# Mixer of a hybrid encoder step on Trainium2: three selection rounds a step for the first scored tile, and one weight split moved behind a group of projections

## The chip, the cores and the metric

The kernel runs on one core of a Trainium2 chip. What counts is the device time of one execution in microseconds (us). The kernel before took 1135.36 us, the median of three runs (1133.62 to 1137.08). One more execution was profiled; every duration of a single instruction below comes from that one.

The engines are named as the profile names them: PE is the matrix engine (its weight loads are listed apart as PEld), DVE the vector engine, ACT the scalar engine, POOL the GpSimd engine, SP the engine whose queue issues most of the DMA transfers.

## The reference, cut to what matters

One encoder layer is computed for 512 prompt tokens and 32 sample tokens that share the weights: a feed-forward block, a mixer, a second feed-forward block, each closed by a layernorm. The change is in the mixer. Its input projection and its sparse attention are, in short:

```python
z = jnp.einsum('btd,de->bte', h, w_in)          # retention q,k,v,gate | attention q,k,v | indexer q, key, head weights
s = jnp.einsum('bqhd,bsd->bqhs', iq, ik) * (IDX_DH ** -0.5)
index_score = jnp.einsum('bqh,bqhs->bqs', iw, jax.nn.relu(s))
index_score = jnp.where(admissible[None], index_score, NEG)
_, idx = lax.top_k(index_score, topk)           # topk = 128 prompt, 136 sample
logits = jnp.einsum('bqhd,bqkhd->bqhk', q, kg) * (ATT_DH ** -0.5)
p = jax.nn.softmax(logits, axis=-1)             # over the selected keys alone
```

Each query token scores all keys that it may see, keeps the best 128 (136 for the sample tokens), and attends to those. Beside it four retention heads run (a chunked recurrence with its own q, k, v).

## The kernel before, in words

**Layout.** Activations lie transposed: 128 partitions of the model width by 544 tokens, in two halves of 272 columns. Every weight is split in two parts (a rounded part and the remainder, "hi" and "lo"), so that a product of a 128 x 1024 weight block with one half is 24 matmuls. PE does these almost without a break; that is where nearly all of the time goes.

**Weights.** A weight block is fetched by SP's queue into a raw tile (`wr_w`, three buffers), rounded by ACT into the hi part (`wh_w`, line 131, five buffers), and the lo part is made in one of two ways: by a subtraction on DVE (line 141), or by ACT (line 138) and an adding DMA that POOL issues (line 139). `ensure(n)` sees to it that n weights ahead of the next one have been split; `next_w` takes the next. The order in which the program asks for a split sets where the fetch stands in SP's queue, where the rounding stands on ACT and where the subtraction stands on DVE. The input projection has 33 weight blocks. The first four (the index key with the head weights, and three of the four index queries) are taken together; the fifth is the last index query; the sixth is the q of the first retention head. The fifth and the sixth have their lo part made on DVE.

**Around the first projections.** The last products of the first feed-forward block (`dn`), the layernorm of each half and the four leading projections overlap. `k_outer` runs the four leading projections together over one half, and lets other jobs go on after every second part of the width. For the second half, the sums S and Q (lines 264 and 265) go through two matmuls (`pm`, `pv`), which PE holds between the first and the second quarter of the leading projections of the first half; then DVE and ACT make the normalised and split input `h` of that half (lines 332 to 367).

**Jobs and steps.** Side work is written as jobs that are resumed at every tick of the program; a tick comes after each product of a block with a half, or so. `topk()` is such a job. It selects in rounds of eight: `max` finds the eight largest of each row (line 1125), `match_replace` marks them in the row (line 1126). Tiles 1, 2 and 3 of 128 queries have rows of 256, 384 and 512 scores and take 16 rounds each; the sample tile 's' has rows of 544 and takes 17. (Tile 0 has 128 keys and needs none.) After its rounds a tile's row is turned into a mask (line 1129) that the attention adds to its logits (line 1293). The `rate` in `topk` is the number of rounds in one step. As the job goes straight on with the next tile, everything behind a tile that is done in fewer steps moves up as well.

**Attention.** `attention()` is another job. For a pair of heads c and a group n of query tiles it forms logits (`lg`) in two PSUM banks, one for each head of the pair; group 0 holds tiles 0 and 1, group 1 tile 2, group 2 tile 3. DVE adds the mask and takes the maximum (line 1293), which frees the bank; ACT and DVE do the softmax (lines 1285 to 1290). The name `lg` has two banks in all, so that the logits of the next group wait until the masks of this group have been added.

**What sets the order.** Instructions of one engine stand in one list, and the rows of the trace start in the order of that list. A scheduler orders the lists when the kernel is built, from the order of the program, priorities and given dependencies. So a change of one number in `topk` moves rows of DVE and ACT over a long stretch.

## Time and profile before

| what | value |
|---|---|
| median of three runs | 1135.36 us |
| lowest and highest run | 1133.62, 1137.08 us |
| the profiled execution's own time | 1134.79 us |
| its span, first to last instruction | 1133.0 us |
| PE busy | 1110.3 us (98%) |
| DVE busy | 850.6 us (75%) |
| ACT busy | 636.8 us (56%) |
| granted PE clock, mean over the span | 0.993 |

A row of the timeline reads: start in us from the start of the span, duration of the row in us, engine, line, operation, out<-in, shape, how many instructions the row merges, and in brackets the idle time of the engine just ahead and what ended it. The table by windows gives for each stretch the busy time of every engine, then the PE clock that was granted (1.00 is full speed), the share of the DMA engines that was busy and GB/s.

### The profile page before, as it was taken

How to read it: one execution, taken by the hardware profiler on the slowest of the kernel's cores; microseconds unless marked ns; L12 is line 12 of the kernel's file. 1: busy time of each engine (PE TensorE's matmuls, PEld its weight loads, DVE VectorE, ACT ScalarE, POOL GpSimd, SP SyncE). 2: the span in 40 equal slices, each digit the busy share in tenths (PEclk: the TensorE clock that was granted, in tenths of full speed). 3: DMA queues.
4: the chain of work that ended last, by engine and by line, in shares of the span. 5: the costliest groups of instructions: out<-in, count | busy, mean ns of one | idle time of the engine just before them, and what ended most of it. 6: DMA issues, size and time to landing. Idle time of an engine off the chain costs nothing.

```text
span 1133.0 us, 22791 instructions
## 1 busy us (share of the span) xinstructions
PE 1110.3 (98%) x9059; PEld 1079.8 (95%) x9059; DVE 850.6 (75%) x1766; ACT 636.8 (56%) x1116; POOL 196.3 (17%) x217
## 2 busy tenths in 40 slices
PE   8999999999999999999989999999999999999995
PEld 7999999999999999989988899999999999999995
DVE  5578898788779799677898887799799876920416
ACT  3645656754334444865556668646666666653524
POOL 0111111122010303422110101100111111151110
PEclk9999999999999999999989999999999999999998
DMA  9798878997977556744946587862888677488842
GB/s 359 274 270 220 224 191 218 260 269 246 320 208 171 143 217 151 155 117 127 276 91 199 123 270 204 206 194 34 231 221 229 167 174 184 129 226 176 175 83 80
DMA packets 71164, 221.18 MB, mean 195 GB/s; under 512 B 8624, under 2 KB 12848, under 8 KB 71056
## 3 DMA queue, kind: packets, MB, share of 16 engines
q1 hardware_dynamic: 49456, 151.02, 37.9%
q0 software_dynamic: 21456, 68.56, 33.6%
q8 instruction: 71, 1.16, 0.4%
q14 instruction: 37, 0.30, 0.1%
q10 hardware_dynamic: 144, 0.14, 0.0%
HBM read 208.09 MB, written 9.58 MB: 192 GB/s over the span
## 4 chain that ended last, share of the span: by engine, by line
PE 86%; DVE 7%; DMA 5%; ACT 1%; issue 1%; SPq 0%; DVEq 0%; ACTq 0%
PE dn L77 26%; PE pA L77 16%; PE in L77 13%; PE gu L77 11%; PE pB L77 8%; PE pC L77 4%; DMA we_raw<-in_w_e 3%; PE gu_e L77 2%; DVE m L1125 1%; DVE wk L1126 1%; DMA aqk<-rp 1%; PE isc L77 1%; PE ro L77 1%; PE lg L77 1%; PE pt L80 1%
## 5 line engine op out<-in xcount | busy, mean ns | idle before, releaser
L77 PE MATMUL dn<-hid,wh_w 128*128 128x272 f32 x2112 | 267.1, 288 | 0.0
L77 PEld LDWEIGHTS dn<-hid,wh_w 128*128 128x128 f32 x2112 | 265.5, 188 | 0.4 <-DMA wh_w<-in_w_dn 0.3
L77 PE MATMUL in<-h,wh_w 128*128 128x272 f32 x1392 | 188.5, 293 | 0.0
L77 PEld LDWEIGHTS in<-h,wh_w 128*128 128x128 f32 x1392 | 178.5, 190 | 5.1 <-issue 2.9
L131 ACT CAST wh_w<-wr_w 128x1024 fp32r<-128x1024 f32 (+1 forms) x102 | 103.0, 1014 | 99.6 <-PE dn L77 83.7
L77 PE MATMUL gu<-h,wh_w 128*128 128x272 f32 x960 | 121.1, 288 | 0.0
L77 PEld LDWEIGHTS gu<-h,wh_w 128*128 128x128 f32 x960 | 120.6, 188 | 0.0
L589 DVE SCALAR_TENSOR_TENSOR ca<-wc,cz,ca 128x1024 f32<-128x1024 f32 x84 | 107.4, 1298 | 0.0
L77 PE MATMUL pA<-hs,wh_s 128*128 128x272 f32 x720 | 100.2, 288 | 0.0
L77 PEld LDWEIGHTS pA<-hs,wh_s 128*128 128x128 f32 x720 | 93.7, 188 | 0.0
L138 ACT ACTIVATE wh_w<-wh_w 128x1024 fp32r<-128x1024 f32 (+1 forms) x80 | 81.5, 1023 | 1.5
L286 DVE SCALAR_TENSOR_TENSOR xs<-dn,C,xs 128x272 f32<-128x272 f32 (+2 forms) x24 | 9.0, 403 | 80.3 <-PE dn L77 80.3
L693 POOL DMA_DIRECT2D wh_g<-in_w_gu x30 | 26.1, 870 | 240.8 <-ACT wh_g L692 164.1
L727 ACT COPY s<-pA 128x272 f32<-128x272 f32 x90 | 34.5, 383 | 53.7 <-PE pA L77 53.1
L139 POOL DMA_DIRECT2D wh_w<-in_w_dn x32 | 28.2, 880 | 174.9 <-ACT wh_w L138 131.8
L716 DVE TENSOR_TENSOR wh_s<-wr_g,wh_s 128x1024 fp32r<-128x1024 f32 x30 | 36.7, 1225 | 19.4 <-ACT wh_s L715 19.4
L77 PE MATMUL pA<-h,wh_g 128*128 128x272 f32 x360 | 50.1, 288 | 0.0
L77 PE MATMUL pB<-hs,wh_u 128*128 128x272 f32 x360 | 49.8, 287 | 0.0
L77 PE MATMUL pC<-h,wh_g 128*128 128x272 f32 x360 | 49.8, 287 | 0.0
L77 PE MATMUL pB<-hs,wh_s 128*128 128x272 f32 x360 | 49.8, 287 | 0.0
L77 PE MATMUL pA<-h,wh_s 128*128 128x272 f32 x360 | 49.7, 287 | 0.0
L715 ACT CAST wh_s<-wr_g 128x1024 fp32r<-128x1024 f32 x30 | 31.5, 1051 | 30.2 <-DVE wr_g L711 30.2
(331 smaller groups left out, 2051.5 us busy)
## 6 DMA issues: line engine op xcount, KB each, us to landing
wc<-in_w_cond SPq DMA_DIRECT2D x52, 512.0 KB, 6.8
wr_w<-in_w_in SPq DMA_DIRECT2D x33, 512.0 KB, 5.2
wr_g<-in_w_gu SPq DMA_DIRECT2D x30, 512.0 KB, 3.5
wr_u<-in_w_gu SPq DMA_DIRECT2D x30, 512.0 KB, 4.4
wh_g<-in_w_gu POOLq DMA_DIRECT2D x30, 512.0 KB, 6.6
wr_w<-in_w_dn SPq DMA_DIRECT2D x32, 448.0 KB, 4.3
wh_w<-in_w_in POOLq DMA_DIRECT2D x27, 512.0 KB, 6.6
wr_w<-in_w_gu SPq DMA_DIRECT2D x24, 512.0 KB, 7.2
```

The lines of the kernel that those rows point to most:

```text
L77: ordered("pe", nc.tensor.matmul(*a, **kw))
L80: ordered("pe", nc.tensor.transpose(*a))
L131: c = nc.scalar.copy(hi[:, :n, :], raw[:, :n, :])
L138: nc.scalar.mul(lo[:, :n, :], hi[:, :n, :].bitcast(F32), -1.0)
L139: nc.gpsimd.dma_start(lo[:, :n, :], src, accum_op=ALU.add)
L589: got = nc.vector.scalar_tensor_tensor(acc, ws[n], c, acc, op0=ALU.mult, op1=ALU.add)
L693: nc.gpsimd.dma_start(lo, src, accum_op=ALU.add)
L715: pin(nc.scalar.copy(W[f][:, 0], raw[f]))
L716: pin(nc.vector.tensor_tensor(W[f][:, 1], raw[f], W[f][:, 0].bitcast(F32), op=ALU.subtract))
L727: pin(nc.scalar.copy(s, ps))
L1125: behind(behind(nc.vector.max(m8, w), "pe"), "norm")
L1126: nc.vector.match_replace(w, in_to_replace=m8, in_values=w, imm_value=MARK)
```

## The change

Three edits. In the mixer's head, `ensure(2)` becomes `ensure(1)`: ahead of the leading projections one weight is split (the fifth), no longer two. Inside the loop over the halves, `ensure(2)` now stands behind `k_outer`, so that the sixth weight is split behind the products of the first half (in the second pass it finds nothing to do). And in `topk`, tile 1 takes three rounds a step where it took two; tiles 2 and 3 keep two, the sample tile keeps its own rhythm.

```diff
     hls = [next_w(0) for c in range(4)]
-    ensure(2)
+    ensure(1)
     misc = unit("misc")
@@
     for i, (a, b) in enumerate(HALVES):
         accs = [(hls[c], bank(("aaao", "lltt")[i][c], "in")[:, :HT]) for c in range(4)]
         k_outer(accs, h, i)
+        ensure(2)
         for c, (_, ps) in enumerate(accs):
             taken((z, *qs)[c])(ps, a, b)
@@
     def topk():
-        for t, rate in ((1, 2), (2, 2), (3, 2), ('s', 1)):
+        for t, rate in ((1, 3), (2, 2), (3, 2), ('s', 1)):
```

No instruction is added or taken out on any engine, and PE's list and POOL's list keep their order. What moves stands on DVE, ACT and SP. (Behind line 1003 the lines of the changed kernel have numbers higher by one.)

**First place: DVE at the layernorm ahead of the projections.** The subtraction for the sixth weight stood between two steps of the layernorm of the first half:

```order
 L265 TENSOR_TENSOR Q<-Q,sq 128x272
 L338 SCALAR_TENSOR_TENSOR pv<-lnz 128x272
-L141 TENSOR_TENSOR wh_w<-wr_w,wh_w 128x1024
 L339 SCALAR_TENSOR_TENSOR pv<-pv,lnz 128x272
 L341 SCALAR_TENSOR_TENSOR lny<-pv,lny 128x272
```

It is gone from there. A little further on in the same list, S and Q are the sums of the second half, h_5 to h_7 the last parts of the input of the first half:

```order
 L367 SCALAR_TENSOR_TENSOR h_4_4815<-ht,B_3755,h_4_4815 128x272
-L364 SCALAR_TENSOR_TENSOR ht<-xa_3229,G_3754,lny 128x272
+L367 SCALAR_TENSOR_TENSOR h_5_4816<-ht,B_3755,h_5_4816 128x272
 L364 SCALAR_TENSOR_TENSOR ht<-xa_3230,G_3754,lny 128x272 x2
-L367 SCALAR_TENSOR_TENSOR h_5_4816<-ht,B_3755,h_5_4816 128x272
+L264 TENSOR_TENSOR S<-S,xa_3230 128x272
+L265 TENSOR_TENSOR Q<-Q,sq 128x272
 L367 SCALAR_TENSOR_TENSOR h_6_4817<-ht,B_3755,h_6_4817 128x272
 L367 SCALAR_TENSOR_TENSOR h_7_4818<-ht,B_3755,h_7_4818 128x272
-L264 TENSOR_TENSOR S<-S,xa_3230 128x272
-L265 TENSOR_TENSOR Q<-Q,sq 128x272
```

S and Q now stand ahead of the last two parts of h; they stood behind them. The subtraction itself comes back behind the first two instructions of a side job (`ca`, the sums of a conditioning vector):

```order
 L607 TENSOR_SCALAR ca_0_4927<-wc_0_4929,cz 128x1024
 L607 TENSOR_SCALAR ca_1_4928<-wc_0_4929,cz 128x1024
+L141 TENSOR_TENSOR wh_w<-wr_w,wh_w 128x1024
 L609 SCALAR_TENSOR_TENSOR ca_0_4927<-wc_1_4930,cz,ca_0_4927 128x1024
 L609 SCALAR_TENSOR_TENSOR ca_1_4928<-wc_1_4930,cz,ca_1_4928 128x1024
```

That is behind the whole layernorm of the second half.

**Second place: SP's queue over the same stretch.** The raw tile of the sixth weight was fetched with the five ahead of it:

```order
-L74 DMA wr_w<-in_w_in 128x1024 x6
+L74 DMA wr_w<-in_w_in 128x1024 x5
 L74 DMA misc<-in_csm 128x12
 L74 DMA misc<-in_cikT 128x512
 L74 DMA tabA<-in_ropes 128x1088
 L74 DMA tabR<-in_ropes 128x1088
-L74 DMA wc_4_4955<-in_w_cond 128x1024
-L74 DMA wc_5_4957<-in_w_cond 128x1024
-L74 DMA wr_w<-in_w_in 128x1024 x4
+L74 DMA wc_4_4950<-in_w_cond 128x1024
+L74 DMA wc_5_4952<-in_w_cond 128x1024
+L74 DMA wr_w<-in_w_in 128x1024 x5
```

It now stands behind the small tables and two conditioning weights, ahead of four other weights.

**Third place: DVE ahead of the first masked logits.** `wk_5279` holds tile 3 here and `wk_5278` the sample tile; aks and aqs are the lo parts of the keys and queries of head pair 0; the last row is the first masking. Before, its last twelve rows were:

```order
L1126 MATCH_REPLACE wk_5279<-m_7099,wk_5279 128x512
L1125 MAX m_7137<-wk_5279 128x8
L1126 MATCH_REPLACE wk_5279<-m_7137,wk_5279 128x512
L1125 MAX m_7140<-wk_5279 128x8
L1125 MAX m_7182<-wk_5278 128x8
L1126 MATCH_REPLACE wk_5279<-m_7140,wk_5279 128x512
L1126 MATCH_REPLACE wk_5278<-m_7182,wk_5278 128x544
L1129 TENSOR_SCALAR wk_5279<-wk_5279 128x512
L1125 MAX m_7185<-wk_5278 128x8
L1132 MEMSET wk_5279 64x64
L1126 MATCH_REPLACE wk_5278<-m_7185,wk_5278 128x544
L1293 ISA Pu,mx<-lg,wk_5279 128x128
```

Now they are:

```order
L1127 MATCH_REPLACE wk_5278<-m_7058,wk_5278 128x544
L962 TENSOR_TENSOR aks<-aqk,aks 128x512
L962 TENSOR_TENSOR aqs<-aqk,aqs 128x512
L1126 MAX m_7116<-wk_5278 128x8
L1127 MATCH_REPLACE wk_5278<-m_7116,wk_5278 128x544
L1126 MAX m_7154<-wk_5278 128x8
L1127 MATCH_REPLACE wk_5278<-m_7154,wk_5278 128x544
L1126 MAX m_7194<-wk_5278 128x8
L1127 MATCH_REPLACE wk_5278<-m_7194,wk_5278 128x544
L1126 MAX m_7197<-wk_5278 128x8
L1127 MATCH_REPLACE wk_5278<-m_7197,wk_5278 128x544
L1294 ISA Pu,mx<-lg,wk_5279 128x128
```

Counted in the two lists from the statistics of the fourth retention head (`bst`) to that first masking: 10 rounds of tile 3 and 2 of the sample tile before, 4 of tile 3 and 6 of the sample tile now. Tile 3 is finished ahead of aks, and four rounds of the sample tile follow on aqs where six and a half of tile 3 and two of the sample tile stood. From the third to the fourth head's statistics the list held 6 rounds of tile 2 and 6 of tile 3, and holds 12 of tile 3 now; the earlier stretches take up the rest, three rounds at a time where two stood.

## The prediction

> **What bounds the kernel now.** I read the page first, then what PE waited for, then PE's own timeline around those waits, and last what DVE did meanwhile.

> ```profile
> span 1133.0 us, 22791 instructions
> PE 1110.3 (98%) x9059; PEld 1079.8 (95%) x9059; DVE 850.6 (75%) x1766; ACT 636.8 (56%) x1116; POOL 196.3 (17%) x217
> PE 86%; DVE 7%; DMA 5%; ACT 1%; issue 1%; SPq 0%; DVEq 0%; ACTq 0%
> PE lg L77 <- DVE mx L1293: 3.5, 2, 3.2
> PE pm L77 <- DVE S L264: 1.5, 1, 1.5
> ```

> PE is busy for 98% of the span and carries 86% of the chain that ended last. Its list and its matmuls stay as they are, so the change can win only what PE waits or runs slowly. The list of what each engine waited for (total, times, longest) has two entries in the mixer of over 1 us for PE, and both are waits for DVE: 3.2 us at the logits (`lg`) and 1.5 us at the layernorm's sums (`pm`).

> First the logits, in PE's timeline and in the windows:

> ```profile
> 582.16 3.26 PE L77 MATMUL in<-h,wh_w 128*128 128x272 f32 x24
> 588.64 1.73 PE L77 MATMUL lg<-aks,aqs 64*128 64x384 f32 x6 [3.22 <-DVE mx L1293]
> 590.30 5.31 PE L77 MATMUL in<-h,wh_w 128*128 128x272 f32 x24
> 612.10 0.80 PE L77 MATMUL lg<-aks,aqs 64*128 64x384 f32 x6
> ...
> 408.00:410.00 2.00, 1.05 (x5) 0.90 (x6) 1.24 (x4) 0.53 (x2) 0.00 (x0) 1.00 1.01 409
> ...
> 588.00:590.00 2.00, 1.36 (x6) 1.10 (x6) 2.00 (x14) 1.72 (x7) 0.00 (x0) 0.51 0.30 57
> 596.00:598.00 2.00, 2.00 (x19) 1.64 (x16) 1.33 (x3) 1.50 (x5) 0.00 (x0) 1.00 0.37 139
> ```

> PE is through at 585.42 and starts the logits of group 1 at 588.64. The wait costs more than its length: behind it the granted clock is 0.51, and 1.00 again in the window from 596. Six logits take 1.73 us where the same six take 0.80 at 612.10, and 24 projections 5.31 us instead of 3.26. So the place costs 3.22 + 0.93 + 2.05 = 6.2 us. The wait of 1.5 us at `pm` left the clock alone (1.00 in the window from 408).

> [...]

> **Why DVE is late there.**

> ```profile
> 562.22 0.49 DVE L1268 BATCH_NORM_STATS2 bst<-rsB 128x6 f32<-128x128 f32 x2 [3.23 <-ACT rsB L1238]
> 575.84 0.69 DVE L962 TENSOR_TENSOR aqs<-aqk,aqs 128x512 fp32r<-128x512 f32 x1 [0.37 <-ACT aqs L961]
> 577.23 0.69 DVE L1125 MAX8 m<-wk 128x8 f32<-128x512 f32 x1
> 578.75 0.69 DVE L1125 MAX8 m<-wk 128x8 f32<-128x512 f32 x1
> 586.22 0.72 DVE L1125 MAX8 m<-wk 128x8 f32<-128x544 f32 x1
> 587.05 0.71 DVE L1126 MATCH_REPLACE8 wk<-m,wk 128x544 f32<-128x544 f32 x1
> 587.68 0.28 DVE L1293 CUSTOM_DVE_ANT_0 Pu<-lg,wk 128x128 f32<-128x128 f32 x1
> 588.16 0.41 DVE L1293 CUSTOM_DVE_ANT_0 Pu<-lg,wk 128x256 f32<-128x256 f32 x1
> 588.57 0.41 DVE L1293 CUSTOM_DVE_ANT_0 Pu<-lg,wk 128x256 f32<-128x256 f32 x1
> ```

> The banks of group 0 come free when its four maskings are done, the first bank at 588.57 and the second at 588.98. DVE begins them at 587.68 because selection rounds stand ahead of them: from the fourth head's statistics at 562.22 it works on without a gap but for the 0.37 us ahead of aqs. It is a queue of work, not a late input.

> **The attention's part, step by step.** A round of tile 3 takes 578.75 - 577.23 = 1.52 us; a round of the sample tile, from the two rows of 544, 587.05 + 0.71 - 586.22 = 1.54 us. By the two lists shown above, the stretch from `bst` to the first masking loses 6 rounds of tile 3 (9.1 us) and gains 4 of the sample tile (6.2 us), and the 0.37 us ahead of aqs goes, since DVE now comes to aqs later than its input: 3.3 us earlier, 584.4. Counted the other way, on from aqs: that had four and a half rounds of tile 3 ahead of it in the stretch, and now has four, two of the sample tile and tile 3's mask (some 0.5 us): 3.1 + 0.5 - 0.8 - 0.4 = 2.4 us later, at 578.2; with its own 0.69 and four rounds the masking starts at 585.1. I take 584.7: the first bank is free at 585.6, the second at 586.0. PE wants the first at 585.42 and the second one matmul later, so about 0.5 us of wait stays, and a wait of three times that has left the clock alone. The logits behind that, at 590.30 + 5.31 = 595.6 before, come at 585.42 + 0.5 + 0.8 + 3.1 = 589.8: a gain of **5.8 us**. The ends: nothing, if DVE is no earlier, and 6.2.

> That DVE has room for the rounds which come earlier is seen in its own waits from 436 to 562:

> ```profile
> DVE rqk L951 <- ACT sw L950: 12.8, 13, 1.9
> DVE bst L1268 <- ACT rsB L1238: 3.7, 3, 1.2
> ...
> 560.33 0.39 PE L77 MATMUL ro<-rv,rqk 128*128 128x128 f32 x2
> ```

> It stood idle for 12.8 us ahead of 13 evacuations and 3.7 us ahead of three statistics, and then 3.23 us ahead of the fourth (the row at 562.22), all of them waits for ACT. Rounds moved up fall into such gaps. Where they don't fit, rows behind them slip: between the third and the fourth statistics six rounds of tile 3 replace six of 384 columns, at most 6 x 1.52 / 4 = 2.3 us more, and 3.23 us of gap stand at the end. The nearest need of PE there is the last state of the retention, used at 560.33 and written by the last DVE row but one ahead of 562.22 - 3.23 = 559.0; 2.3 us on top would make PE wait some 0.7 us. Part of it goes into the gaps, so I take 0; the ends are 0 and 0.7. And aqs, done at 578.9, is asked for at 581.28 (a row below): 2.4 us of cover.

> What is late next: DVE has gained 3 us there, PE 5.8, so their next meeting tightens.

> ```profile
> 581.28 0.95 PE L77 MATMUL lg<-aks,aqs 64*128 64x128 f32 x12
> 596.67 0.17 DVE L1289 RECIPROCAL rl<-l 128x1 f32<-128x1 f32 x1 [1.58 <-ACT Pu L1287]
> 604.54 0.68 DVE L962 TENSOR_TENSOR aqs<-aqk,aqs 128x512 fp32r<-128x512 f32 x1
> 606.18 0.95 PE L77 MATMUL lg<-aks,aqs 64*128 64x128 f32 x12
> 639.31 1.19 PE L77 MATMUL lg<-aks,aqs 64*128 64x384 f32 x6 [0.26 <-DVE mx L1293]
> ```

> PE wants head pair 1 at 606.18 - 5.8 = 600.4. DVE's list from the first masking to that aqs is as before: 605.22 - 587.68 = 17.5 us, with 1.58 us in it for an exponential that stood on ACT behind an evacuation of the slow PE block. In ACT's new list the evacuation stands behind it, so 15.9 us: ready at 600.6. With the handing over I take **0.5 us** lost; the ends are 0 and, with the 1.58 us kept, 1.8. The wait of 0.26 us at 639.31 goes, since the sample tile's last rounds no longer stand ahead of it: **0.3 us** won.

> **The layernorm's part.**

> ```profile
> 391.88 12.52 PE L77 MATMUL dn<-hid,wh_w 128*128 128x272 f32 x96
> 404.24 3.18 PE L77 MATMUL in<-h,wu_w 128*128 128x272 f32 x24
> 408.95 0.73 PE L77 MATMUL pm<-S,cm 128*128 128x272 f32 x2 [1.52 <-DVE S L264]
> ...
> 399.15 1.22 DVE L141 TENSOR_TENSOR wh_w<-wr_w,wh_w 128x1024 fp32r<-128x1024 f32 x1
> 400.29 0.44 DVE L339 SCALAR_TENSOR_TENSOR pv<-pv,lnz 128x272 f32<-128x272 f32 x1
> 407.22 1.32 DVE L367 SCALAR_TENSOR_TENSOR h<-ht,B,h 128x272 fp32r<-128x272 f32 x3
> 408.46 0.43 DVE L264 TENSOR_TENSOR S<-S,xa 128x272 f32<-128x272 f32 x1
> ```

> PE has done its first 24 projections at 407.42 and waits until 408.95 for S, which ends at 408.89. The subtraction at 399.15 holds DVE's list up by 400.29 - 399.15 = 1.14 us, and two of the three h rows at 407.22 now stand behind S, 0.83 us. Without both S could end at 406.9. It also needs the last `dn` product, which PE ends at 404.40; from there two updates, two rows of h and the two ahead of h follow, six rows of at most 0.41 us, and S itself: 407.3 at the latest. That is ahead of 407.42, so **1.5 us** go. The ends: 0, if something else holds the list, and 1.5, since no more is waited.

> The subtraction and the fetch are paid later.

> ```profile
> 403.80 21.07 SPq L74 DMA_DIRECT2D wr_w<-in_w_in  x4
> 430.37 1.48 SPq L1010 DMA_DIRECT2D rp<-ix  x2
> 426.82 12.04 DVE L609 SCALAR_TENSOR_TENSOR ca<-wc,cz,ca 128x1024 f32<-128x1024 f32 x10
> ```

> With all 1.5 us earlier, DVE is through `ca`'s first two rows at 425.3 and the subtraction at 426.5, while PE comes to the sixth weight behind ten blocks of 24 from 404.24 on, at about 436. It lies beside PE's work and costs nothing: 9 us of cover. In SP's queue the fetch of the ninth weight waits for that subtraction (for the raw buffer), and the index key's gathers (line 1010) stand behind it. Before, the fourth of the fetches at 403.80 was out by 424.87; now the last two go out at 426.5, ahead of 428.9, when the gathers are due.

> **The sum**, against the profiled 1134.79 us: - 5.8 - 1.5 + 0.5 - 0.3 = - 7.1, so 1127.7. The median stands 0.6 above that execution: **1128.3 us** is the forecast.

> **The rivals.**

> The wait moves to head pair 1: 1.8 us remain there, or the clock falls as well. With the clock kept the time is 1.3 more, 1129.6; halved, it is another 0.93 + 2.05, 1132.6. For it: both engines meet there within 0.2 us by the sum above. Against: such a wait is nearer to the 1.52 us that left the clock alone. Chance 0.10, half for each.

> The rounds do nothing for PE, and only the layernorm's 1.5 us come: 1133.9. For it: the stretch starts with a wait for ACT that the change leaves in place. Against: DVE idles no more than 0.37 us in the 25 us behind it. Chance 0.06.

> The half clock fell on the profiled execution and not on most of the timed ones. A before without it loses 3.2 us at the logits and not 6.2, so the gain is 3.0 smaller: 1131.3. The three runs lie 3.5 us apart, which fits either way. Chance 0.06. [...]

> Slower: SP's queue now depends on DVE. If the moved subtraction ended late, the fetch that waits for its buffer would hold the gathers behind it, and with them the index scores and every round. It would have to end behind all of `ca`, 426.82 + 12.04 = 438.9, which makes the gathers 10 us late; what covers the first microseconds is not in these rows, so I count 4 us of it, and PE waits 6 us with a halved clock behind, 9 us in all: 1137.3. It decides from about 433 on. The list puts the subtraction ahead of ten of the twelve `ca` rows, so 0.04.

> The change does what the sum says: 0.74, with 1126 to 1130 as its own range.

> **How the numbers follow.** Faster by over 0.3% (3.4 us, about what a measurement of this kernel tells from no change) is below 1132.0: the forecast's 0.74, 1129.6 (0.05) and 1131.3 (0.06), less 0.01 for spread: 0.84. Within 0.3%: 1132.6, 1133.9 and that rest, 0.12. Slower: 0.04. The range 1125.5 to 1132.0 leaves out those 0.16 above; its low end is the sum with all 6.2 us, without the 0.5, and 1.7 us for the distance of the lowest run from the median.

> **What would show it.** Right: no wait of PE over 0.6 us at `lg` or `pm`; the clock at 1.00 all through the mixer; the first masking begun at most 0.5 us ahead of PE's call for the bank; aqs of pair 1 the next wait, under 1 us. Wrong: a clock near 0.5 anywhere between 570 and 640, a wait of PE at `ro` or at the first `lg`, or the gathers of line 1011 begun behind 429.

## The result

The changed kernel takes 1126.94 us (median of five runs, 1126.58 to 1128.46) beside 1136.76 us for the kernel before (five runs): a ratio of 0.9922, with a 95% interval of 0.9907 to 0.9938. Two later comparisons of the same pair gave 0.9933 (0.9920 to 0.9945) and 0.9942 (0.9929 to 0.9956). The forecast was 1128.3 with a range of 1125.5 to 1132.0. The profiled execution took 1126.58 us. One of the five runs in the last of these comparisons took 1342.37 us at a granted clock of 0.751 and is left out of every figure here.

From the page of the changed kernel, and then from the list of what PE waited for (total, times, longest):

```profile
span 1124.7 us, 22790 instructions
PE 1107.7 (98%) x9059; PEld 1077.4 (96%) x9059; DVE 848.5 (75%) x1766; ACT 637.4 (57%) x1116; POOL 196.1 (17%) x217
PE idle L77 <- POOL zeros L496: 1.2, 1, 1.2
PE c L77 <- DVE modT L523: 0.7, 1, 0.7
PE pt L80 <- ACT Pu L1414: 0.6, 1, 0.6
```

The span is 8.3 us shorter. Both entries of the mixer that named DVE, 3.5 us at `lg` and 1.5 us at `pm`, are gone from the list; what is left of the mixer there is 0.6 us for ACT at `pt`, which the kernel before had too. Next PE's timeline at the places that the prediction spoke of, and two stretches of the table by windows (the PE clock is the third number from the end):

```profile
404.35 3.19 PE L77 MATMUL in<-h,wu_w 128*128 128x272 f32 x24
407.37 0.62 PE L77 MATMUL pm<-S,cm 128*128 128x272 f32 x2
580.45 3.26 PE L77 MATMUL in<-h,wh_w 128*128 128x272 f32 x24
583.83 1.20 PE L77 MATMUL lg<-aks,aqs 64*128 64x384 f32 x6
584.96 3.30 PE L77 MATMUL in<-h,wh_w 128*128 128x272 f32 x24
598.83 0.95 PE L77 MATMUL lg<-aks,aqs 64*128 64x128 f32 x12
631.63 0.79 PE L77 MATMUL lg<-aks,aqs 64*128 64x384 f32 x6
...
584.00:586.00 2.00, 2.00 (x14) 1.52 (x15) 2.00 (x13) 1.71 (x7) 0.00 (x0) 1.00 1.06 162
588.00:590.00 2.00, 2.00 (x17) 1.44 (x16) 2.00 (x8) 1.94 (x6) 0.00 (x0) 1.00 0.00 0
```

PE's list is the same in both kernels, so one matmul can be followed from trace to trace. `pm` starts at 407.37 where it started at 408.95. The logits of group 1 start at 583.83 (588.64), those of head pair 1 at 598.83 (606.18), those of group 1 of head pair 2 at 631.63 (639.31). So the lead over the kernel before is 1.6 us behind the layernorm, 4.8 us when the banks come free, 7.35 us at head pair 1 and 7.7 us at head pair 2. The clock is 1.00 all through the mixer, and the 24 projections behind the logits take 3.30 us, not 5.31.

Last DVE, with the rows that answer to those shown of before:

```profile
406.74 0.44 DVE L264 TENSOR_TENSOR S<-S,xa 128x272 f32<-128x272 f32 x1
424.04 1.22 DVE L141 TENSOR_TENSOR wh_w<-wr_w,wh_w 128x1024 fp32r<-128x1024 f32 x1
560.51 0.49 DVE L1269 BATCH_NORM_STATS2 bst<-rsB 128x6 f32<-128x128 f32 x2 [2.26 <-ACT rsB L1239]
576.05 0.69 DVE L962 TENSOR_TENSOR aqs<-aqk,aqs 128x512 fp32r<-128x512 f32 x1
582.87 0.28 DVE L1294 CUSTOM_DVE_ANT_0 Pu<-lg,wk 128x128 f32<-128x128 f32 x1
583.76 0.41 DVE L1294 CUSTOM_DVE_ANT_0 Pu<-lg,wk 128x256 f32<-128x256 f32 x1
598.06 0.68 DVE L962 TENSOR_TENSOR aqs<-aqk,aqs 128x512 fp32r<-128x512 f32 x1
```

From the fourth head's statistics to the first masking DVE took 587.68 - 562.22 = 25.5 us before and takes 582.87 - 560.51 = 22.4 us now. PE asks for the first bank at 580.45 + 3.26 = 583.71; the second is released at 584.17. What is left of the wait lies there: 0.12 us ahead of the row at 583.83, and 0.40 us inside it (1.20 us against 0.80 for the same six matmuls), 0.5 us in all.

### The profile page after: what moved, and what is told of

Its sections match the earlier page's. It is cut to its first block, busy times and chain, and to the rows that moved or that the text cites. A ratio compares the mean times of both kernels' runs of the same rounds, so it can differ in the third digit from the quotient of the medians.

```text
span 1124.7 us, 22790 instructions
## 1 busy us (share of the span) xinstructions
PE 1107.7 (98%) x9059; PEld 1077.4 (96%) x9059; DVE 848.5 (75%) x1766; ACT 637.4 (57%) x1116; POOL 196.1 (17%) x217
## 4 chain that ended last, share of the span: by engine, by line
PE 89%; DVE 5%; DMA 4%; issue 1%; ACT 1%; SPq 0%; DVEq 0%; POOL 0%; POOLq 0%; ACTq 0%
PE dn L77 26%; PE pA L77 16%; PE in L77 16%; PE gu L77 11%; PE pB L77 8%; PE pC L77 4%; DMA we_raw<-in_w_e 3%; PE gu_e L77 2%; PE pt L80 1%; PE po L77 1%; PE lg L77 1%; PE isc L77 1%; DMA wh_w<-in_w_dn 1%; PE ro L77 1%; DVE m L1126 1%
## 5 line engine op out<-in xcount | busy, mean ns | idle before, releaser
L77 PE MATMUL dn<-hid,wh_w 128*128 128x272 f32 x2112 | 267.0, 288 | 0.1
L77 PEld LDWEIGHTS dn<-hid,wh_w 128*128 128x128 f32 x2112 | 265.5, 188 | 0.5 <-DMA wh_w<-in_w_dn 0.3
L77 PE MATMUL in<-h,wh_w 128*128 128x272 f32 x1392 | 186.5, 291 | 0.0
L77 PEld LDWEIGHTS in<-h,wh_w 128*128 128x128 f32 x1392 | 176.4, 188 | 4.9 <-issue 2.9
L77 PE MATMUL gu<-h,wh_w 128*128 128x272 f32 x960 | 121.1, 288 | 0.0
L77 PEld LDWEIGHTS gu<-h,wh_w 128*128 128x128 f32 x960 | 120.6, 188 | 0.0
L77 PE MATMUL pA<-hs,wh_s 128*128 128x272 f32 x720 | 100.3, 288 | 0.0
L77 PEld LDWEIGHTS pA<-hs,wh_s 128*128 128x128 f32 x720 | 93.7, 188 | 0.0
L77 PE MATMUL pA<-h,wh_g 128*128 128x272 f32 x360 | 50.1, 288 | 0.0
L77 PE MATMUL pB<-hs,wh_u 128*128 128x272 f32 x360 | 49.8, 287 | 0.0
L77 PE MATMUL pC<-h,wh_g 128*128 128x272 f32 x360 | 49.8, 287 | 0.0
L77 PE MATMUL pB<-hs,wh_s 128*128 128x272 f32 x360 | 49.8, 287 | 0.0
L77 PE MATMUL pA<-h,wh_s 128*128 128x272 f32 x360 | 49.7, 287 | 0.0
```

What stands on the lines that cost most here:

```text
L77: ordered("pe", nc.tensor.matmul(*a, **kw))
```

## Experiments

All times are medians; the ratio is to the kernel before, run beside each group on the same chip (1134.60, 1134.88 and 1134.49 us in the three groups).

| kernel | us | ratio (95%) |
|---|---|---|
| both (the change) | 1126.64 | 0.9933 (0.9920 to 0.9945) |
| weight_only | 1133.19 | 0.9990 (0.9981 to 0.9999) |
| rounds_only | 1129.53 | 0.9955 (0.9942 to 0.9967) |
| weight_later | 1128.77 | 0.9947 (0.9933 to 0.9960) |
| masks_4 | 1129.60 | 0.9953 (0.9940 to 0.9967) |
| masks_8 | 1133.01 | 0.9985 (0.9975 to 0.9995) |
| tile2_instead | 1127.98 | 0.9939 (0.9925 to 0.9952) |
| vector_splits | 1127.29 | 0.9932 (0.9919 to 0.9944) |
| both_again (the change) | 1128.05 | 0.9942 (0.9929 to 0.9956) |
| tile3_instead | 1134.16 | 0.9999 (0.9990 to 1.0008) |
| tile1_four | 1127.14 | 0.9935 (0.9923 to 0.9947) |
| four_and_splits | 1126.29 | 0.9930 (0.9916 to 0.9943) |

### The two parts, each alone

The change itself, once more:

> The changed kernel itself, beside the two that follow. The two profiles differ by 8.3 us (1133.0 and 1124.7 of span). If that is all that the change does, the time falls by 8.3 us, with 7.5 to 9.1 for the spread of the medians. If part of the 9.8 us between the two medians measured so far is real, some 1.5 us come from something that the two profiles do not show.

Measured: 8.0 us less than the kernel before, within what was expected. Nothing here asks for more than the 8.3 us of the two profiles; the 9.8 us between the first two medians are not repeated.

The weight alone:

```diff
-    ensure(2)
+    ensure(1)
@@
         k_outer(accs, h, i)
+        ensure(2)
```

> Only the two edits on the sixth weight; tile 1 keeps two rounds a step. The theory of the prediction: the wait of 1.52 us for S goes and nothing else, so 1.7 us less than the kernel before (the two profiles are 1.66 us apart at that point), and the wait of 3.2 us at the logits of group 1 stays as long as it was, with the granted clock near 0.5 behind it. Rival: DVE is tied to something there that does not come earlier, so that PE, 1.7 us earlier, waits 4.9 us at the logits and the time does not move.

The rounds alone:

```diff
-        for t, rate in ((1, 2), (2, 2), (3, 2), ('s', 1)):
+        for t, rate in ((1, 3), (2, 2), (3, 2), ('s', 1)):
```

> Only the third edit: three rounds a step in tile 1; the sixth weight is split where it was. The theory of the prediction: 3.1 us of wait at the logits and 2.7 us of half clock go, and some 0.5 us at the logits of group 1 of head pair 2, so 6.2 to 6.6 us less than the kernel before; the wait of 1.5 us for S stays. Rival, that the half clock fell on the profiled execution and not on most timed ones: 3.0 us less of a gain, 3.5 us. With the other kernel the gains add up to that of both edits, to within 1 us.

Measured: 1.4 us less for the weight, 5.1 us less for the rounds, 6.5 us together against 8.0 for both edits. That is 1.5 us apart where 1 us was expected, and the rounds alone gave 1.1 us less than the 6.2 expected; the intervals allow equality (the product of the two ratios is 0.9945). PE's timeline of weight_only and then of rounds_only around the logits, and of the same two at `pm` of the first half:

```profile
588.35 1.73 PE L77 MATMUL lg<-aks,aqs 64*128 64x384 f32 x6 [3.21 <-DVE mx L1294]
590.00 5.14 PE L77 MATMUL in<-h,wh_w 128*128 128x272 f32 x24
...
588.10 1.20 PE L77 MATMUL lg<-aks,aqs 64*128 64x384 f32 x6
...
392.50 0.73 PE L77 MATMUL pm<-S,cm 128*128 128x272 f32 x2 [1.68 <-DVE S L264]
...
392.47 0.75 PE L77 MATMUL pm<-S,cm 128*128 128x272 f32 x2 [1.73 <-DVE S L264]
```

With the weight alone the wait at the logits is 3.21 us, as before, and the clock is at 0.50 behind it: DVE and PE both come earlier by what the layernorm won, and the rival (a wait of 4.9 us) is out. With the rounds alone the wait ahead of the logits is gone. A gain of 3.5 us, as the rival has it in which the half clock fell on the profiled execution alone, lies outside the interval (3.7 to 6.6 us). The mean granted clock of the timed runs points the same way: 0.993 or 0.994 in 13 of the 15 runs of the kernel before and 0.995 in two; 0.996 or 0.997 in ten of the 14 runs of the changed one and 0.995 in four. The 6.8 us at half speed in 1133 take 0.003 off the mean. The mean also holds the slow clock at the start of the kernel, which lasts 4.4 to 10.4 us in the profiles, so a single 0.995 does not tell which it was.

But both profiles hold a wait that neither edit explains: 1.7 us at `pm` of the first half, near 391, where the kernel before and the changed kernel have none. It is taken up below (vector_splits). In rounds_only's profiled execution, the slowest of its five, that place costs 3.5 us against the changed kernel's trace: 1.9 of waiting and 1.6 of half clock behind it. How many of the other runs have it is not known.

### Does DVE's list alone decide?

Rows added to DVE's list ahead of the maskings that free the banks (k is 4, then 8):

```diff
+                    for _ in range(k if (c, n, t) == (0, 0, 0) else 0):
+                        masked(Pt, ps[:, a:b], work[t], mx)
                     masked(Pt, ps[:, a:b], work[t], mx)
```

> The changed kernel, with the masking of tile 0 of head pair 0 done four times more for each head of the pair (the same sums into the same place): eight more rows, which start 0.21 us apart in the profile of the changed kernel, ahead of the two maskings that free the banks. They add 1.7 us to DVE's list between PE's first logits and the logits of group 1, and nothing else moves on DVE. The theory: DVE's list alone decides when PE gets the banks, so the wait of 0.5 us there becomes 2.2 us and the time rises by 1.7 us over the changed kernel, or by up to 3 us more where the granted clock falls behind it. Rival: rows ahead of the masking are taken up by a gap or another wait, so that the time rises by under 0.5 us and the gain of the change came from elsewhere.

> The same with eight more maskings for each head, sixteen rows, 3.4 us. The theory: a wait of 3.9 us at the logits of group 1, with the clock near 0.5 behind it as in the kernel before: 3.4 us of wait and 2.5 to 3 us of slow matmuls, 6 to 6.5 us over the changed kernel, which is its whole gain at this place given back. If the clock stays at 1.00, it is 3.4 us. Rival as before: under 1 us.

Measured: 0.9953 and 0.9985 against 0.9933, so 2.3 and 5.9 us more than the change. PE's timeline of masks_4, then of masks_8, and a window of masks_8:

```profile
585.41 1.19 PE L77 MATMUL lg<-aks,aqs 64*128 64x384 f32 x6 [1.81 <-DVE mx L1294]
586.53 3.26 PE L77 MATMUL in<-h,wh_w 128*128 128x272 f32 x24
...
586.60 1.73 PE L77 MATMUL lg<-aks,aqs 64*128 64x384 f32 x6 [3.50 <-DVE mx L1294]
588.26 5.48 PE L77 MATMUL in<-h,wh_w 128*128 128x272 f32 x24
...
588.00:590.00 2.00, 2.00 (x10) 1.74 (x8) 2.00 (x11) 0.20 (x2) 0.00 (x0) 0.50 0.00 0
```

The wait grows by the rows that were added: 0.12, 1.81, 3.50 us for none, eight and sixteen of them, 0.21 us for each. At 1.81 us the clock stays at 1.00 and 24 projections take 3.26 us; at 3.50 us it falls to 0.50 and they take 5.48. Held against the trace of the changed kernel, masks_8 loses 3.4 us by waiting and 2.7 us by the clock. That is close to what the prediction priced the place at (3.22 + 2.98), put back by hand.

### Is it the tile, or the stretch?

```diff
-        for t, rate in ((1, 3), (2, 2), (3, 2), ('s', 1)):
+        for t, rate in ((1, 2), (2, 3), (3, 2), ('s', 1)):     # tile2_instead
+        for t, rate in ((1, 2), (2, 2), (3, 3), ('s', 1)):     # tile3_instead
```

> The changed kernel with tile 1 back at two rounds a step and tile 2 at three. DVE's list from the fourth head's statistics to the first masking holds the same rows as in the changed kernel (four rounds of tile 3, then six of the sample tile), while the stretches ahead of it differ: from the third to the fourth statistics one round of tile 2 and twelve of tile 3 where the changed kernel has twelve of tile 3. The theory, that it is the number of rounds in this last stretch that counts and not the tile that was made faster: the same wait of 0.5 us at the logits of group 1, no half clock, and the same time as the changed kernel to within 0.5 us. Rival, that the last state of the retention now comes too late: 1.2 us more on DVE ahead of it, against 2.3 us of idle time in front of the fourth statistics in the changed kernel, so a wait of PE at ro of 0 to 1.2 us.

> The changed kernel with tile 1 back at two rounds a step and tile 3 at three. From the fourth head's statistics to the first masking DVE's list holds ten rounds as in the changed kernel (seven of tile 3 and three of the sample tile), so the wait at the logits of group 1 should be the same 0.5 us. But from the third to the fourth statistics it holds six rounds of tile 2 (1.2 us each) and nine of tile 3 (1.52 us) where the changed kernel has twelve of tile 3: 20.9 against 18.2 us, 2.6 us more. This is the place that the prediction named as a risk: the last state of the retention stood ready 0.7 us ahead of PE's matmul that takes it (558.26 and 558.93), so PE waits up to 1.9 us at ro, and the time is that much above the changed kernel's. The other theory: the 2.6 us fall into DVE's waits for ACT in that stretch, PE does not wait at ro, and the time is that of the changed kernel to within 0.5 us.

Measured: 0.9939 for tile 2, not told apart from the change; 0.9999 for tile 3, no gain over the kernel before at all. PE's timeline of tile2_instead, then of tile3_instead, then DVE's of tile3_instead with the four maskings of group 0 and two of the rows between them:

```profile
584.49 1.19 PE L77 MATMUL lg<-aks,aqs 64*128 64x384 f32 x6
...
587.60 0.68 PE L77 MATMUL lg<-aks,aqs 64*128 64x384 f32 x1 [3.85 <-DVE mx L1294]
589.52 1.32 PE L77 MATMUL lg<-aks,aqs 64*128 64x384 f32 x5 [1.24 <-DVE mx L1294]
...
583.61 0.28 DVE L1294 CUSTOM_DVE_ANT_0 Pu<-lg,wk 128x128 f32<-128x128 f32 x1
583.82 0.72 DVE L1126 MAX8 m<-wk 128x8 f32<-128x544 f32 x1
...
584.51 0.28 DVE L1294 CUSTOM_DVE_ANT_0 Pu<-lg,wk 128x128 f32<-128x128 f32 x1
...
585.54 0.72 DVE L1126 MAX8 m<-wk 128x8 f32<-128x544 f32 x1
...
587.13 0.41 DVE L1294 CUSTOM_DVE_ANT_0 Pu<-lg,wk 128x256 f32<-128x256 f32 x1
...
589.04 0.42 DVE L1294 CUSTOM_DVE_ANT_0 Pu<-lg,wk 128x256 f32<-128x256 f32 x1
```

With tile 2 faster the place looks as it does in the change: no wait ahead of the row, and 0.4 us inside it. With tile 3 faster I expected the same 0.5 us at the logits and a wait at `ro`. Neither came. PE does not wait at `ro`: the last state that PE takes there is written by 557.48 and asked for at 558.66, and the added rounds stand behind it, in the gap that was ahead of the fourth statistics. (The row that ends at 558.26 in the changed kernel, on which the expectation rests, writes the state that leaves by DMA.) At the logits the first masking starts at 583.61, only 0.7 us later than in the change, but three rounds of the sample tile stand between the four maskings, so that the last for each bank starts at 587.13 and 589.04, where in the change all four are done within 1.3 us. PE loses 3.85 and 1.24 us, and the clock with them (0.50 from 587 to 593). I had counted the rounds ahead of the first masking and not what the new order puts among the four; the bank is free behind the last.

### A subtraction that ends late

```diff
         k_outer(accs, h, i)
-        ensure(2)
+        ensure(2 if i else 1)
```

> The changed kernel with the sixth weight's split asked for behind the second half of the leading projections, no longer behind the first. DVE's list is the same but for the subtraction, which moves behind all twelve rows of ca; SP's list is the same. The rival that the prediction counted as slower, put to the test: the subtraction ends near 437.2 us, the fetch of the ninth weight waits for it, and the gathers behind that fetch go out at some 438, 9.5 us later than now. The rope and the lo parts of the index queries would follow by 9 us, to 456, where PE asks for them at 451: a wait of 5 to 6 us, with the half clock behind it 8 to 9 us more than the changed kernel, that is about as slow as the kernel before. The other theory: the queue does not hold the gathers, and PE waits only for the weight itself, 436 to 437.2: 1.2 us more than the changed kernel.

Measured: 0.9947 against 0.9933, 2.1 us more than the change by the medians. PE's timeline, SP's queue and what SP waited for between 403 and 432, of weight_later; the last two rows are SP's queue and its waits (403 to 430) in the changed kernel:

```profile
438.67 15.06 PE L77 MATMUL in<-h,wh_w 128*128 128x272 f32 x118 [0.90 <-DVE wh_w L141]
405.11 22.90 SPq L74 DMA_DIRECT2D wr_w<-in_w_in  x5
430.19 1.24 SPq L1011 DMA_DIRECT2D rp<-ix  x2
SPq L74 <- ACT wh_w L131: 10.0, 2, 8.4
...
428.70 1.33 SPq L1011 DMA_DIRECT2D rp<-ix  x2
SPq L74 <- DVE wh_w L141: 0.6, 1, 0.6
```

PE waits 0.90 us for the weight itself, 1.2 us of lead lost at that matmul, and the gathers go out at 430.19, late by 1.5 us, which is what PE itself is late there (the wait near 391, 1.58 us, is in this profile too). So the second theory describes this run. But the rival was not put to the test as I had meant: in the changed kernel the last of the five fetches waits for the subtraction, and in this one the fetches wait for ACT and not for the subtraction. What a late subtraction costs while the fetch is tied to it stays open.

### The wait that comes and goes

```diff
     for c in range(4):
-        queue_w(w_in[c], lo_eng=nc.gpsimd if c else nc.vector, pool=up)
+        queue_w(w_in[c], lo_eng=nc.vector, pool=up)
```

> The changed kernel, with the subtractions for the second, third and fourth projection weight on DVE, no longer on POOL (three rows of 1.2 us on DVE for three of 2.4 us on POOL). In three of the profiles so far PE waits 1.6 to 1.7 us at pm near 392, in the others not at all. Where it waits, POOL's first subtraction had started 0.1 us ahead of DVE's for the first weight, which then took 3.4 us in place of 1.2; the fetch that waits for that raw buffer went out 2 us later and landed 6 us later, and POOL's other two subtractions fell beside DVE's S, which took 2.1 us in place of 0.4. The theory, that the two engines keep each other out: with the subtractions on DVE alone none of its rows takes over 1.3 us there, the third fetch is out by 377 in every execution, PE never waits at pm near 391, and the times lie at the lower edge of the changed kernel's (1126.2 to 1127.4) with none near 1128.5. Rival, that the late landing comes by itself: the wait shows now and then all the same, and the spread stays.

The two subtractions that meet, in the changed kernel (DVE, then POOL) and in rounds_only (DVE, POOL, and DVE's sum of the first half), and last the same sum and DVE's subtractions in vector_splits:

```profile
375.39 1.22 DVE L141 TENSOR_TENSOR wu_w<-wr_w,wu_w 128x1024 fp32r<-128x1024 f32 x1
375.54 3.33 POOL L141 TENSOR_TENSOR wu_w<-wr_w,wu_w 128x1024 fp32r<-128x1024 f32 x1 [1.39 <-DVE red L553]
...
375.08 3.45 DVE L141 TENSOR_TENSOR wu_w<-wr_w,wu_w 128x1024 fp32r<-128x1024 f32 x1
375.06 2.40 POOL L141 TENSOR_TENSOR wu_w<-wr_w,wu_w 128x1024 fp32r<-128x1024 f32 x1 [1.22 <-ACT wu_w L131]
390.34 2.07 DVE L264 TENSOR_TENSOR S<-S,xa 128x272 f32<-128x272 f32 x1
...
376.08 2.35 DVE L141 TENSOR_TENSOR wu_w<-wr_w,wu_w 128x1024 fp32r<-128x1024 f32 x2
390.65 0.44 DVE L264 TENSOR_TENSOR S<-S,xa 128x272 f32<-128x272 f32 x1
```

In both traces the one that starts first takes its usual time (1.22 us on DVE, 2.40 on POOL), and the other one takes nearly the rest of that on top: the first still has 2.38 us to go in rounds_only and 1.07 in the changed kernel, and the second takes 2.23 and 0.93 us longer than alone, the same to within 0.15 us. What holds the second one back is not shown.

Of the twelve profiles with POOL's subtractions, seven have DVE ahead, by 0.01 to 0.17 us, and no wait near 391 (this includes the kernel before and three of the change). Four have POOL ahead by 0.02 to 0.12 us (weight_only, rounds_only, weight_later, tile1_four), and 1.4 to 1.7 us of wait: DVE's subtraction takes 2.2 us longer, the third weight is fetched 2 us later and lands near 386 and not near 380, so that POOL's other two subtractions fall beside DVE's S. The order of the transfers may account for the further 4 us: POOL, done sooner, issues its next adding DMA (line 139) at 377.85 in rounds_only, ahead of that fetch at 378.62, where in the changed kernel it goes out at 378.82, behind the fetch at 376.69. No run tests that. In the last, tile2_instead, POOL is 1.3 us ahead and PE waits 0.85 us. None of the edits touches this place. In the two profiles with all subtractions on DVE no row there takes over 1.24 us and PE doesn't wait.

The time does not show it: 0.9932 (1126.06 to 1129.19), the same as the change, and the spread stays, as the rival had it, though the wait itself is not in the profile. So the delay is shown in the profiles, and its share in the timed runs is not.

The change once more, beside the last group:

> The changed kernel once more, as the measure for the three beside it: 7.5 to 8.5 us less than the kernel before.

Measured: 0.9942, 6.4 us less by the medians and so below the 7.5 expected; the interval, 5.0 to 8.1 us, reaches into what was expected. The profiled execution took 1129.29 us and shows another source of the spread, in PE's timeline behind the mixer:

```profile
708.45 0.39 PE L77 MATMUL shp<-shr,onesr 128*128 128x272 f32 x1 [1.28 <-ACT shr L235]
```

Up to 700 it is within 0.4 us of the first one; behind this wait and what follows it, it is 2.7 us late.

### A better version?

```diff
-        for t, rate in ((1, 3), (2, 2), (3, 2), ('s', 1)):
+        for t, rate in ((1, 4), (2, 2), (3, 2), ('s', 1)):
```

> The changed kernel with four rounds a step in tile 1. From the fourth statistics to the first masking DVE's list holds nine rounds where it held ten, only two and a half of them behind aqs, six and a half ahead of it where six stood. The theory: masking begins 1.5 us earlier, and the 0.5 us that PE still loses at the logits of group 1 in the changed kernel goes; aqs is a round later, done at 578.2, ahead of PE's call at 579.5. No wait comes at head pair 1, since masking and PE both come earlier there by DVE's 1.5 and PE's 0.5 us. So 0.5 us less than the changed kernel. Rival: aqs or another row becomes late and PE waits there for about as much: no change.

> Four rounds a step in tile 1 and the three subtractions on DVE, on top of the changed kernel: the attempt at a better version. The 0.5 us at the logits and, in the executions that have it, the 1.7 us at pm near 391: the median 0.5 to 1.0 us below the changed kernel, the upper edge of the runs 1.5 us below. Rival: the spread comes from elsewhere, the start of the kernel above all, and the median moves by under 0.5 us.

Measured: 0.9935 and 0.9930, neither told apart from the change. PE's timeline of tile1_four:

```profile
578.80 3.27 PE L77 MATMUL in<-h,wh_w 128*128 128x272 f32 x24 [0.50 <-ACT aqk L928]
586.06 0.79 PE L77 MATMUL lg<-aks,aqs 64*128 64x384 f32 x6
```

The 0.4 us inside the logits are gone, as expected, and 0.5 us of waiting for an evacuation on ACT come 7 us earlier: the rival. Counted from the statistics the first masking came 0.7 us earlier and not 1.5, since by the trace nine and a half rounds stood ahead of it and not nine. With three and with four rounds a step the rest at this place is moved and not won.

## Why the prediction was right

**The logits, - 5.8.** The two traces give - 5.6 between the last matmul ahead of the logits and the block behind them: 3.1 us of wait, 0.5 in the logits and 2.0 in the 24 projections. The 0.2 us between the two figures is the block behind the logits, taken as 3.1 us where the prediction's own rows have 3.26 and the trace 3.30. The three parts are those that the prediction read from one profile, and masks_8 brought them back by a delay alone. The stretch on DVE was shortened by 3.1 us; the two counts gave 3.3 and 2.6 (587.68 less 585.1). In the kernel before, five and a half rounds of tile 3 stood behind aqs, as the second count has it, and not the six and a half of the text on the change. The rest of 0.5 us was forecast and is 0.5. One sign was set too narrowly: the first masking began 0.8 us ahead of PE's call, where at most 0.5 was named, though the prediction's own times are 0.7 apart.

**The layernorm, - 1.5.** It is - 1.7. S starts at 406.74 and ends at 407.18, within the 406.9 to 407.3 that were worked out, ahead of PE's call.

**Head pair 1, + 0.5.** This term failed: PE does not wait. aqs is done at 598.74 and asked for at 598.83. DVE took 598.74 - 582.87 = 15.9 us from the first masking to there, as forecast; but the masking began 0.3 us ahead of the time I took (584.7 less the 1.5 us of the layernorm is 583.2, and it began at 582.87), and nothing was lost in handing over. The chain of steps was right, but its result was a small difference of two large terms, smaller than their errors. The margin left is 0.1 us.

**Head pair 2, - 0.3.** It is - 0.7. The 0.26 us in brackets were only what stood ahead of the row; inside it the second bank was waited for as well (1.19 us for six matmuls that take 0.8). The prediction's own rows show that difference (1.19 and 0.80), and it was not priced.

**The cover at the retention.** At most 2.3 us of slip were allowed for, against 1.3 us of cover. The cover was larger: the last state that PE takes was written by 558.13 and not 559.0 (the row behind it writes the state that leaves by DMA), 2.2 us ahead of 560.33. In the changed kernel it is written by 557.39 and asked for at 558.62; against PE's timeline, which is 1.7 us earlier, that is about 1 us of slip, and no wait.

**SP's queue.** The gathers were out at 428.70, ahead of 428.9, as forecast; but only the last of the five fetches waits for the subtraction (0.6 us), not the last two.

The sum was - 7.1 against 8.3 us measured between the spans: 0.5 that was not lost at head pair 1, 0.4 more at head pair 2, and 0.2 more at the layernorm, with the 0.2 less at the logits against it; the rest, 0.2 to 0.3, lies behind 660. Three of these errors point the same way, and the sum stayed near the result because each was small. The low end of the range adds up to 1125.7, not 1125.5. Of the rivals, "the rounds do nothing" and "the half clock fell on the profiled execution alone" are out by rounds_only; "the wait moves to head pair 1" did not happen, by 0.1 us; the one on the slower side did not happen either, and its price is untested.

## What to carry to other kernels

Price a wait of PE with the slow matmuls behind it, from the windows of the same profile: here 3.2 us of waiting cost 6.2. When rows are moved in a list that is short of time, count up to the last instruction that releases the buffer, not to the first, and read the new order between them, since a rate that looks equivalent can put work in there (tile3_instead). Two engines that meet within 0.2 us, as DVE and POOL do near 375, can leave a wait in one profile and none in the next (1.4 to 1.7 us in four of the twelve here, none in seven): look at the same row in several.

## What was not expected of the hardware

The clock fell behind a short wait. The table by windows for rounds_only at 391, behind the wait of 1.73 us:

```profile
391.00:392.00 1.00, 0.00 (x0) 0.00 (x0) 1.00 (x1) 0.00 (x0) 1.00 (x1) 1.00 0.76 295
393.00:394.00 1.00, 1.00 (x4) 0.74 (x4) 0.38 (x3) 0.67 (x2) 0.00 (x0) 0.52 0.00 0
395.00:396.00 1.00, 1.00 (x7) 1.00 (x6) 1.00 (x3) 0.00 (x0) 0.00 (x0) 0.50 0.00 0
398.00:400.00 2.00, 2.00 (x18) 2.00 (x17) 1.82 (x5) 1.98 (x4) 0.00 (x0) 1.00 0.00 0
```

PE was back at 392.47 and worked at half speed from 393.0 to 396.4, 3.4 us. Behind waits of 1.58, 1.68 and 1.81 us in other profiles (weight_later, weight_only, masks_4) the clock stayed at 1.00, so the length alone does not decide. In the kernel before, weight_only, masks_8 and tile3_instead, where PE stood for 3.2 us and more, it was at 0.50 for 6.8 us each time (588.05 to 594.9 in the kernel before), twice as long, and it fell 2.2 to 3.3 us after PE had stopped.
